# Rotary buffers and gathered v in a pool of their own, w_out staging moved, and the last stores of a hybrid encoder block in another order

## The chip, the cores and the metric

The kernel runs on one core of one Trainium2 chip. Its time is the device time of one execution in microseconds, and the median of several runs counts. The engines are named as in the profile: PE is TensorE's matmuls and PEld its weight loads, DVE is VectorE, ACT is ScalarE, POOL is GpSimd, SP is SyncE, which only issues DMAs. Each engine works through its own queue in order; engines wait for each other through semaphores.

## The reference

One layer: a projection into heads of two kinds, attention in both, a gate, a projection back, and a layer norm.

```python
h = x @ w_in                                   # 1024 x 1024 by 1024 x 3328
q_a, k_a, v_a, z_a, q_b, k_b, v_b, z_b = split(h)
y_a = neighborhood_attention(q_a, k_a, v_a, rel_bias)      # 8 heads, 8 x 16 windows on a 16 x 64 grid
y_b = windowed_gqa_with_sink(rotary(q_b), rotary(k_b), v_b, sink)   # 8 query heads, 2 kv heads, |i - j| <= 128
mixed = concat([y_a * silu(z_a), y_b * silu(z_b)])
x = layer_norm(ALPHA * x + mixed @ w_out) * gain + bias    # over rows of 1024, ALPHA = 2 ** 0.25
```

All inputs and the output are float32. x and the output are 1024 rows of 1024.

## The kernel before

Every large product is done in float16 pieces: an operand is scaled by a power of two and split into a high and a low half, and three matmuls (high by high, high by low, low by high) are summed in PSUM. The scale of a weight comes from the data, so weights are read twice in part: once for a sum of absolute values, once for the work.

The program falls into three stages.

**The head** computes v = x @ w_v for all tokens (`v_mms`, first four token tiles in float32r, the other four in float16 pieces) and then projects the first six column groups (`project`, ORDER[:6] = zb0, z0, kb, zb1, qb0, z1). It runs inside a `with` block that owns two pools, `vp` and `vw`; when the block is left their memory is free for the pools opened next. `vp` holds, in this order, the staging of x (tag `xr`, four buffers of 2 KB per partition) and two rings of three 2.6 KB buffers (tags `wvr` and `vt`), used first for raw w_v and then for the split v that is written to DRAM (`v_part`, L774, tile `vt`, DRAM tensor `vd`). `vw` holds eight tiles `v32` of 2.5 KB with v in float32, and then sixteen 2.5 KB tiles `wvh0`, `wvl0`, `wvh1`, ... `wvl7` with the split w_v. The last are read by the matmuls of the first phase alone, k = 7 last. `t_load` puts four raw blocks of w_out (`wot`) into such tiles, `t_add` combines them, and `t_store` writes the sums to DRAM (`tf`, L637).

The order of side work in the head is written by hand: `at(c, fn)` registers a function that runs after the c-th projection matmul, 48 matmuls for a group, 24 for each half of the tokens. `run_to` pumps matmuls and fires these events. `sum_w(i)` (L790, with its load at L724) sums the absolute values of the i-th of the 15 later weight groups, `w_scan` (L267) does so for the first six groups, and `w_scale(n)` turns the sums into a scale: one small matmul against ones (L273) and a chain of one-element operations on VectorE (L274 to L293). `w_scale(6)` serves all 15 later groups. `w_split` makes the halves of a weight: `hi` on ScalarE (L247), `lo` on GpSimd in two operations (L252, L253); each `lo` releases the next weight load on SP (L236). `wo_load` and `wo_scan` (L1043, L1049) read w_out for its scale.

The rotary embedding is `rope`: ScalarE copies a projected half into `rp_raw` (L383), VectorE shuffles it into `rp_sw` (L384), then two multiplies and an add (L385 to L387). Both are buffers of tag `va`. The result is split into keys (`split_k`, tiles `ks`) or queries (`split_q`, tiles `qs`).

Before the kb group ends, the pools are opened that follow `vp` and `vw` in the same memory: `rawp` (12 KB per partition), then `kq`. `kq` holds three tags: `va` (six buffers of 4.1 KB: rotary work here, later the gathered v, the bias tables and some blocks of w_out), `ks` (eight of 2 KB) and `qs` (two of 4 KB). Within a pool the tags lie in the order of their first use, so in `kq` it is `va`, `ks`, `qs`. `reuse_waits="tile"` makes a tile wait only for those earlier tiles whose memory it covers. After `kq` comes `ap` with the working tiles of the attention.

**The live stage** runs 128 attention units with the projections of the other 15 groups interleaved between them (`pump_to`), and a planner that places elementwise work on the engines by estimated costs and due times. Its order of instructions is fixed when the program is built.

**The end** (`final`) multiplies the gated heads by w_out in a scheme of seven products per 2 x 2 blocks, adds x (`add`, L1336), gathers row statistics (`bn`, L1348) and normalises eight blocks of 128 rows. Block t is done by `norm(t)`: for t = 7 ScalarE normalises all 1024 columns at once (L1414), then GpSimd multiplies by the gain (L1425), adds the bias (L1426) and SP stores the half (L1427), which is `norm_half`, called for both halves. The last block is row block 3 (`norm_last`): its right 512 columns and columns 384 to 511 go over VectorE (L1387, L1391) with stores on SP (L1393, L1395), its first 384 columns are multiplied by the gain on GpSimd (`norm_ahead`, L1367), then go through TensorE: an identity matmul (L1374) and two with the diagonal tiles `dm` and `ds` (L1383, L1384), and ScalarE, which also issues their store (L1394, L1396). Between the last product and these, TensorE runs matmuls on a tile of zeros (`warm`, L1373). The calls stand in this order at the end:

```python
c11(3)
norm_ahead(3)
norm_half(7, slice(0, 512))
norm_half(7, slice(512, 1024))
for c, tag in ((0, 256), "t"), ((256, 128), "s"), ((384, 128), "t"):
    add(3, 1, run("q3", 3, bank(tag), None, c), c, whole=True)
norm_last(3)
```

Of the kernel before, what the change touches and what calls it, by code (L numbers as in the profile page):

```python
# [7 lines left out]
F32 = mybir.dt.float32  # L8
# [4 lines left out]
AF = mybir.ActivationFunctionType  # L13
# [18 lines left out]
NPRO = 6  # L32
# [38 lines left out]
def hybrid_block(ctx, tc, xT, x, wt, wv, wo, bias, sink, gain, lbias, cos, sin, bmask, out):  # L71
    nc = tc.nc
# [10 lines left out]
    def bank(tag):  # L83
        bufs = {"pj": 2, "s": 4, "t": 2}[tag]
        return (ps1 if bufs == 1 else ps2).tile([128, 512], F32, tag=tag, name=f"ps_{tag}", bufs=bufs)
# [7 lines left out]
    def big_tile(name, shape=(128, 2, 512), dt=F32R):  # L93
        n = taken[0]
        taken[0] += 1
        tag = "big" if n < 8 or 16 <= n < 24 or n >= 32 + NS else "big2"
        return big.tile(list(shape), dt, tag=tag, name=name)

    xh, xl, x16h, x16l = {}, {}, {}, {}
    for half in range(2):  # L100
        for k in range(KT):
            t = big_tile(f"x{half}{k}", dt=F32 if half else F32R)
# [43 lines left out]
    raws, parts, tiles = {}, {}, {}  # L146
# [29 lines left out]
    def enq(eng, fn, *deps, prio=1, after=0, cost=None):  # L176
        op = Op(eng, fn, deps, prio, cost)
        if clock["step"] is not None:
            queues[eng].append(op)
        elif after:  # L180
            events.setdefault(ran[0] + after, []).append(op.emit)
        else:
            op.emit()
        return op
# [192 lines left out]
    def rope(ps, half):  # L377
        live = clock["step"] is not None
        sl = slice(512 * half, 512 * half + 512)
        eng, mul = ("pool", nc.gpsimd) if live else ("dve", nc.vector)  # L380
        raw = tiles["kq"].tile([128, 1024], F32, tag="va", name="rp_raw", bufs=6)[:, :512]
        sw = tiles["kq"].tile([128, 1024], F32, tag="va", name="rp_sw", bufs=6)[:, :512]
        o1 = enq("act", lambda: nc.scalar.activation(raw, ps, AF.Copy, scale=QSCALE), prio=0)  # L383
        o2 = enq("dve", lambda: nc.vector.stream_shuffle(sw, raw, SWAP), o1, after=2)  # L384
        o3 = enq(eng, lambda: mul.tensor_mul(raw, raw, tiles["cos"][:, sl]), o2, after=3)  # L385
        o4 = enq(eng, lambda: mul.tensor_mul(sw, sw, tiles["sin"][:, sl]), o2, after=3)
        o5 = enq(eng, lambda: mul.tensor_add(raw, raw, sw), o3, o4, after=4)  # L387
        return raw, o1, o5
# [86 lines left out]
    with ExitStack() as vctx:  # L475
        vp = vctx.enter_context(tc.tile_pool(name="vp", bufs=2))
        vw = vctx.enter_context(tc.tile_pool(name="vw", bufs=1))
# [146 lines left out]
        wot = {}  # L624

        def t_load():
            for n in range(4):
                t = vw.tile([128, 640], F32, tag=f"wv{'hl'[n % 2]}{n // 2}", name="wot")
                wot[n] = t[:, :512]
                nc.sync.dma_start(wot[n], wo[3, :, n])  # L630

# [163 lines left out]
        def at(c, fn, *a):  # L795
            events.setdefault(c, []).append(lambda: fn(*a))
# [5 lines left out]
            at(30 + 8 * t, v_part, t)  # L802
        for i in range(NS):
            at(14 + 14 * i + {11: 6, 13: -2, 14: -16}.get(i, 0), sum_w, i)
        at(224, w_scale, NPRO)
        for c, o in zip((20, 28, 68, 76), T_SUM):
            at(c, t_add, *o)
        at(90, t_store)
# [4 lines left out]
    rawp = ctx.enter_context(tc.tile_pool(name="rawp", bufs=1, reuse_waits="tile"))  # L813
    actx = ExitStack()
    tiles["kq"] = ctx.enter_context(tc.tile_pool(name="kq", bufs=4, reuse_waits="tile"))
    ap = actx.enter_context(tc.tile_pool(name="ap", bufs=3, reuse_waits="tile"))
    tiles["ap"] = ap

# [12 lines left out]
    va = {}  # L831

    def big_ap(shape, dt, name):
        return tiles["kq"].tile(shape, dt, tag="va", name=name, bufs=6)

    def gather_v(p):
        t = va[p] = big_ap([128, 8, 4 * VE], F16, f"va{p}")
# [479 lines left out]
    def final():  # L1317
# [15 lines left out]
        def add(t, a, ps, c=(0, 512), whole=False):  # L1333
            o, w = c
            xv = xrs[t][:, 512 * a + o:512 * a + o + w]
            nc.vector.scalar_tensor_tensor(xv, ps[:, o:o + w], yc, xv, op0=ALU.mult, op1=ALU.add)  # L1336
            finish()
            if whole:
                bn(t, a, c)
# [10 lines left out]
        def row_stats(t):  # L1350
            mv = fp.tile([128, 2], F32, tag="mv", name="mv")
            nc.vector.bn_aggr(mv, stats[t][:, :8 if t == 3 else 2, :])
            sd = fp.tile([128, 1], F32, tag="sd", name="sd")
            nc.scalar.activation(sd, mv[:, 1:2], AF.Sqrt, bias=eps)
            return mv, sd

        def row_scale(mv, sd):
            rstd = fp.tile([128, 1], F32, tag="rstd", name="rstd")
            nc.vector.reciprocal(rstd, sd)
            nmr = fp.tile([128, 1], F32, tag="nmr", name="nmr")  # L1360
            nc.vector.tensor_scalar(nmr, mv[:, 0:1], rstd, -1.0, op0=ALU.mult, op1=ALU.mult)
            return rstd, nmr
# [3 lines left out]
        def norm_ahead(t):  # L1366
            nc.gpsimd.tensor_mul(xrs[t][:, HP], xrs[t][:, HP], gb[:, HP])  # L1367

        def norm_last(t):
            ts = slice(128 * t, 128 * t + 128)  # L1370
            xr, pn = xrs[t], bank("t")
            for _ in range(40):
                nc.tensor.matmul(gq[:, :128], warm, warm, start=True, stop=True)  # L1373
            nc.tensor.matmul(pn[:, HP], identf, xr[:, HP], start=True, stop=False)  # L1374
            dm, ds = (fp.tile([128, 128], F32, name=n, bufs=1) for n in ("dm", "ds"))
            mv = fp.tile([128, 2], F32, tag="mv", name="mv")
            nc.vector.bn_aggr(mv, stats[t])
            sd = fp.tile([128, 1], F32, tag="sd", name="sd")
            nc.scalar.activation(dm, nident, AF.Copy, scale=mv[:, 0:1])
            nc.scalar.activation(sd, mv[:, 1:2], AF.Sqrt, bias=eps)  # L1380
            nc.scalar.activation(ds, identf, AF.Copy, scale=sd)
            rstd = fp.tile([128, 1], F32, tag="rstd", name="rstd")
            nc.tensor.matmul(pn[:, HP], dm, gb[:, HP], start=False, stop=False)  # L1383
            nc.tensor.matmul(pn[:, HP], ds, bb[:, HP], start=False, stop=True)  # L1384
            halves = (H1, gp, bp), (HQ, gq[:, 128:256], gq[:, 256:384])
            for h, g, _ in halves:
                nc.vector.scalar_tensor_tensor(xr[:, h], xr[:, h], mv[:, 0:1], g, op0=ALU.subtract, op1=ALU.mult)  # L1387
                if h is H1:
                    nc.vector.reciprocal(rstd, sd)
            for h, _, o in halves:  # L1390
                nc.vector.scalar_tensor_tensor(xr[:, h], xr[:, h], rstd, o, op0=ALU.mult, op1=ALU.add)  # L1391
                if h is H1:
                    nc.sync.dma_start(out[ts, h], xr[:, h])  # L1393
            nc.scalar.activation(xr[:, HP], pn[:, HP], AF.Copy, scale=rstd)  # L1394
            nc.sync.dma_start(out[ts, HQ], xr[:, HQ])  # L1395
            nc.scalar.dma_start(out[ts, HP], xr[:, HP])  # L1396
# [10 lines left out]
        def norm(t, *st_):  # L1407
            ts = slice(128 * t, 128 * t + 128)
            xr, ha, hb = xrs[t], slice(512, 1024), slice(0, 512)
            mv, sd = st_ or row_stats(t)  # L1410
            rstd, nmr = row_scale(mv, sd)
            both = t in (0, 4, 7)
            h = slice(0, 1024) if both else hb
            nc.scalar.activation(xr[:, h], xr[:, h], AF.Identity, bias=nmr, scale=rstd)  # L1414
            if not both:
                nc.vector.scalar_tensor_tensor(xr[:, ha], xr[:, ha], mv[:, 0:1], gp, op0=ALU.subtract, op1=ALU.mult)
                nc.vector.scalar_tensor_tensor(xr[:, ha], xr[:, ha], rstd, bp, op0=ALU.mult, op1=ALU.add)
                nc.sync.dma_start(out[ts, ha], xr[:, ha])
            for h in (ha, hb) if both else (hb,):
                if t != 7:  # L1420
                    norm_half(t, h)

        def norm_half(t, h):
            xr = xrs[t]
            nc.gpsimd.tensor_mul(xr[:, h], xr[:, h], gb[:, h])  # L1425
            nc.gpsimd.tensor_add(xr[:, h], xr[:, h], bb[:, h])  # L1426
            nc.sync.dma_start(out[128 * t:128 * t + 128, h], xr[:, h])  # L1427

# [52 lines left out]
        def c11(t):  # L1481
            add(t, 0, a[t], whole=True)
# [41 lines left out]
        p4(3)  # L1524
        q2(3)
        c11(3)
        norm_ahead(3)
        norm_half(7, slice(0, 512))
        norm_half(7, slice(512, 1024))
        for c, tag in ((0, 256), "t"), ((256, 128), "s"), ((384, 128), "t"):  # L1530
            add(3, 1, run("q3", 3, bank(tag), None, c), c, whole=True)
        norm_last(3)

    def m_last(between):
        z, za = zt[ZP[3][1]], zt[ZP[3][0]]
# [42 lines left out]
    for i in range(-LD, NU + LO):  # L1578
# [5 lines left out]
        per, h = divmod(i, 16)  # L1584
# [5 lines left out]
        if i in SCAN_LD:  # L1590
            n, b = divmod(NSCAN + SCAN_LD.index(i), 4)
# [9 lines left out]
        if i in B_LD:  # L1601
            n = B_LD.index(i)
            b_load(n, w_ops[NL - 5 + n] if n < 5 else b_ops[n - 5])
        if i in B_AT:
            n = B_AT.index(i)
# [51 lines left out]
        if 0 <= q < NU // 4:  # L1657
            g, p, j, h = quad(q)
# [93 lines left out]
```

## Time and profile before

| | |
|---|---|
| median of 3 runs | 440.08 us (439.59 to 440.48) |
| the profiled execution | 442.68 us, of which its span is 440.8 us |
| TensorE busy | 429.9 us (98%), 3209 matmuls |
| VectorE, ScalarE, GpSimd busy | 351.8, 316.3, 293.9 us |
| granted TensorE clock | 1.0 |
| DMA | 84.82 MB moved, mean 192 GB/s |

The profile page gives the busy time of each engine, its course in 40 slices, the DMA queues, the chain of waits that ended last, and the costliest groups of instructions. Times in the timeline are microseconds from the start of the span. Its rows give the start, the length, the engine, the line in the kernel, the operation, the tile written and those read, and their shapes; in brackets stands the time that the engine sat idle before and what ended that. A row of the chain gives start, length and what. Matmuls overlap each other in the pipeline: one of 512 columns lasts 0.38 us but the next starts after 0.22.

### The profile page before, as it was taken

The numbers are of one execution on the slowest core, as the hardware profiler recorded it, in microseconds if no ns is written. First come the engines' busy times: TensorE is split into PE (matmuls) and PEld (weight loads), VectorE is DVE, ScalarE is ACT, GpSimd is POOL, SyncE is SP. The second block draws the span as 40 slices with busy tenths as digits, with TensorE's granted clock in tenths as the row PEclk, the third lists the DMA queues.
The fourth block names the chain that finished last, engine by engine and source line by source line (L and its number), as shares of the span: only waits on it lengthen the run. The fifth ranks groups of instructions, "written<-read, shape, count | busy, mean of one in ns | idle before, by whom it ended". The sixth has DMA issues, their size and how long they took to land.

```text
span 440.8 us, 9457 instructions
## 1 busy us (share of the span) xinstructions
PE 429.9 (98%) x3209; PEld 250.9 (57%) x3209; DVE 351.8 (80%) x872; ACT 316.3 (72%) x682; POOL 293.9 (67%) x303
## 2 busy tenths in 40 slices
PE   9999999999999999999999999999999999999994
PEld 8997754444445655555565555555555655444453
DVE  5978966784987797898898998887888877787684
ACT  5849789669659887878897778879688883653122
POOL 0110085769468746978998899697689899358245
PEclk9999999999999999999999999999999999999999
DMA  7952479995448999988789999977999999923123
GB/s 259 406 187 60 124 236 331 259 328 192 134 141 175 197 159 237 189 166 147 126 188 198 221 191 185 235 176 136 241 177 210 159 169 293 402 86 137 48 75 117
DMA packets 131409, 84.82 MB, mean 192 GB/s; under 512 B 97568, under 2 KB 106656, under 8 KB 131360
## 3 DMA queue, kind: packets, MB, share of 16 engines
q1 hardware_dynamic: 131216, 84.02, 78.9%
q8 instruction: 25, 0.41, 0.4%
q14 instruction: 24, 0.20, 0.1%
q10 hardware_dynamic: 144, 0.20, 0.1%
HBM read 50.60 MB, written 10.52 MB: 139 GB/s over the span
## 4 chain that ended last, share of the span: by engine, by line
PE 58%; DVE 11%; issue 8%; ACT 8%; DMA 7%; POOL 6%; SPq 1%; POOLq 0%; DVEq 0%; ACTq 0%
PE ps_pj L449 21%; PE ps_s L556 6%; PE ps_t L991 5%; PE ps_pj L1300 5%; PE ps_t L1300 4%; PE ps_s L1300 4%; DMA wor<-in_wo 3%; PE ps_pj L556 3%; PE ps_t L556 3%; PE ps_s L914 2%; PE ps_s L915 2%; POOL wl L253 2%; DVE split L963 2%; ACT ps_s L944 1%; DMA T<-td 1%
## 5 line engine op out<-in xcount | busy, mean ns | idle before, releaser
L449 PE MATMUL ps_pj<-xf,wh 128*128 128x512 f16 x672 | 201.3, 379 | 0.3 <-DVE z L414 0.3
L449 PE MATMUL ps_pj<-xf,wl 128*128 128x512 f16 x336 | 127.3, 379 | 0.0
L449 PEld LDWEIGHTS <-wh 128*128 128x128 f16 x672 | 63.7, 98 | 59.8 <-issue 1.8
L944 ACT ACTIVATE ps_s<-sn,nm 128x321 f32<-128x321 f32 (+3 forms) x128 | 67.7, 529 | 35.4 <-DVE nm L928 34.4
L963 DVE SCALAR_TENSOR_TENSOR split<-ps_s,split 128x320 f16<-128x320 f32 (+2 forms) x128 | 62.7, 490 | 23.3 <-ACT split L962 22.1
L252 POOL TENSOR_SCALAR wr<-wr,wsc 128x512 f32<-128x512 f32 x32 | 23.7, 741 | 61.6 <-ACT wh L247 59.0
L962 ACT ACTIVATE split<-ps_s 128x320 f16<-128x320 f32 (+2 forms) x128 | 55.0, 430 | 1.6
L449 PEld LDWEIGHTS <-wl 128*128 128x128 f16 x336 | 32.8, 98 | 38.0
L253 POOL TENSOR_TENSOR wl<-wr,wh 128x512 f16<-128x512 f32 x32 | 39.9, 1247 | 2.7
L914 PE MATMUL ps_s<-ks,qs 128*128 128x320 f16 (+3 forms) x128 | 38.1, 298 | 1.7 <-DVE split L963 1.7
L915 PE MATMUL ps_s<-ks,qs 128*128 128x320 f16 (+3 forms) x128 | 38.2, 298 | 0.0
L991 PEld LDWEIGHTS <-tr 128*128 128x128 f16 (+1 forms) x1056 | 36.2, 98 | 3.3 <-issue 1.2
L928 DVE CUSTOM_DVE_ANT_0 sn<-ps_s,bias,sg 128x368 f32<-128x368 f32 (+1 forms) x64 | 36.1, 564 | 2.1 <-PE ps_s L915 2.0
L928 DVE CUSTOM_DVE_ANT_0 sn<-ps_s,bm,nsk 128x320 f32<-128x320 f32 (+2 forms) x64 | 36.5, 571 | 0.4
L1300 PEld LDWEIGHTS <-m 128*128 128x128 f16 x186 | 17.6, 98 | 19.9 <-POOL m L1222 0.5
L366 POOL COPY ks<-ks 64x512 f16<-64x512 f16 x40 | 25.8, 644 | 3.9 <-ACT ks L310 1.7
L1425 POOL TENSOR_TENSOR xr<-xr,gb 128x512 f32<-128x512 f32 x10 | 12.7, 1270 | 20.2 <-ACT xr L1414 20.2
L247 ACT ACTIVATE wh<-wr,wsc 128x512 f16<-128x512 f32 x32 | 22.7, 710 | 1.6 <-DVE wsc L277 1.6
L556 PEld LDWEIGHTS <-xf 128*128 128x128 f16 x192 | 18.6, 98 | 7.3
L915 PEld LDWEIGHTS <-qs 128*128 128x128 f16 x128 | 12.5, 98 | 17.4 <-issue 3.2
L914 PEld LDWEIGHTS <-qs 128*128 128x128 f16 x128 | 12.5, 98 | 15.2 <-DVE qs L318 0.2
L991 PE MATMUL ps_t<-va,tr 128*128 128x65 f16 (+1 forms) x528 | 19.2, 193 | 0.3 <-DMA tr<-split 0.3
(262 smaller groups left out, 949.1 us busy)
## 6 DMA issues: line engine op xcount, KB each, us to landing
wr<-in_wt SPq DMA_DIRECT2D x32, 256.0 KB, 3.3
ws<-in_wt SPq DMA_DIRECT2D x15, 512.0 KB, 6.5
wor<-in_wo SPq DMA_DIRECT2D x20, 256.0 KB, 3.9
xr<-in_x SPq DMA_DIRECT2D x8, 512.0 KB, 9.1
out<-xr SPq DMA_DIRECT2D x15, 256.0 KB, 2.0
bias<-in_bias SPq DMA_DIRECT2D x8, 440.0 KB, 4.4
wob<-in_wo SPq DMA_DIRECT2D x12, 256.0 KB, 4.0
wvraw<-in_wv SPq DMA_DIRECT2D x9, 320.0 KB, 5.6
```

What stands on the lines that cost most here:

```text
L253: nc.gpsimd.tensor_sub(l, raw, h)
L366: nc.gpsimd.tensor_copy(place(t, o, half, col), place(t, a, half, col))
L449: nc.tensor.matmul(ps, a[:, k % 4, :], mv, start=(k == 0 and i == 0), stop=(k == KT - 1 and i == 2))
L556: nc.tensor.matmul(ps[:, :320], lh[:, ts], rh[:, cs], start=(k == ko[0] and i == 0), stop=(k == ko[-1] and i == 2))
L914: nc.tensor.matmul(ps[:, :n], q, sl[0], start=True, stop=False)
L915: nc.tensor.matmul(ps[:, :n], q, sl[1], start=False, stop=True)
L928: nc.vector.tensor_tensor_reduce(sn[:, at0:at0 + n], ps[:, :n], bias_t, sg[:, c:c + 1], init, op0=ALU.add, op1=ALU.min, accum_out=nm)
L944: nc.scalar.activation(pt[:, c], sn[:, c], AF.Exp, bias=nm, scale=-1.0, accum_out=acc)
L962: nc.scalar.activation(h, pt[:, c], AF.Copy, scale=PSCALE)
L963: nc.vector.scalar_tensor_tensor(l, pt[:, c], PSCALE, h, op0=ALU.mult, op1=ALU.subtract)
L991: nc.tensor.matmul(ps[:, w * m:w * m + e], a, b_, start=(i == 0), stop=(i == len(mms) - 1))
L1300: nc.tensor.matmul(ps[:, cs], lh[:, 128 * t:128 * t + 128], rh[:, cs], start=(fresh and e == 0 and n == 0), stop=(e == len(terms) - 1 and ...
```

## The change

Five edits go together.

1. The tag `va` moves from `kq` into a pool of its own, `va`, which is opened right after `kq`. `kq` then holds keys and queries alone, at the start of the freed memory behind `rawp`, and the rotary buffers lie above them. The sum of both is as large as `kq` was.
2. The raw w_out blocks `wot` are loaded into the tiles of `wvh6`, `wvl6`, `wvh7` and `wvl7` in place of those of `wvh0` to `wvl1`.
3. `w_scale` for the 15 later groups runs after matmul 217 of the head, not after 224.
4. For block 7, ScalarE normalises columns 0 to 511 and 512 to 1023 in two operations, the left ones first. `norm_ahead(3)` stands between the multiply and the add of block 7's left half, and the right half of block 7, its store included, comes behind `norm_last(3)`.
5. `norm_last` runs 28 warm matmuls, not 40.

```diff
--- before.py
+++ after.py
@@ -378,8 +378,8 @@
         live = clock["step"] is not None
         sl = slice(512 * half, 512 * half + 512)
         eng, mul = ("pool", nc.gpsimd) if live else ("dve", nc.vector)
-        raw = tiles["kq"].tile([128, 1024], F32, tag="va", name="rp_raw", bufs=6)[:, :512]
-        sw = tiles["kq"].tile([128, 1024], F32, tag="va", name="rp_sw", bufs=6)[:, :512]
+        raw = tiles["va"].tile([128, 1024], F32, tag="va", name="rp_raw", bufs=6)[:, :512]
+        sw = tiles["va"].tile([128, 1024], F32, tag="va", name="rp_sw", bufs=6)[:, :512]
         o1 = enq("act", lambda: nc.scalar.activation(raw, ps, AF.Copy, scale=QSCALE), prio=0)
         o2 = enq("dve", lambda: nc.vector.stream_shuffle(sw, raw, SWAP), o1, after=2)
         o3 = enq(eng, lambda: mul.tensor_mul(raw, raw, tiles["cos"][:, sl]), o2, after=3)
@@ -625,7 +625,7 @@
 
         def t_load():
             for n in range(4):
-                t = vw.tile([128, 640], F32, tag=f"wv{'hl'[n % 2]}{n // 2}", name="wot")
+                t = vw.tile([128, 640], F32, tag=f"wv{'hl'[n % 2]}{6 + n // 2}", name="wot")
                 wot[n] = t[:, :512]
                 nc.sync.dma_start(wot[n], wo[3, :, n])
 
@@ -802,7 +802,7 @@
             at(30 + 8 * t, v_part, t)
         for i in range(NS):
             at(14 + 14 * i + {11: 6, 13: -2, 14: -16}.get(i, 0), sum_w, i)
-        at(224, w_scale, NPRO)
+        at(217, w_scale, NPRO)
         for c, o in zip((20, 28, 68, 76), T_SUM):
             at(c, t_add, *o)
         at(90, t_store)
@@ -813,6 +813,7 @@
     rawp = ctx.enter_context(tc.tile_pool(name="rawp", bufs=1, reuse_waits="tile"))
     actx = ExitStack()
     tiles["kq"] = ctx.enter_context(tc.tile_pool(name="kq", bufs=4, reuse_waits="tile"))
+    tiles["va"] = ctx.enter_context(tc.tile_pool(name="va", bufs=6, reuse_waits="tile"))
     ap = actx.enter_context(tc.tile_pool(name="ap", bufs=3, reuse_waits="tile"))
     tiles["ap"] = ap
 
@@ -831,7 +832,7 @@
     va = {}
 
     def big_ap(shape, dt, name):
-        return tiles["kq"].tile(shape, dt, tag="va", name=name, bufs=6)
+        return tiles["va"].tile(shape, dt, tag="va", name=name, bufs=6)
 
     def gather_v(p):
         t = va[p] = big_ap([128, 8, 4 * VE], F16, f"va{p}")
@@ -1369,7 +1370,7 @@
         def norm_last(t):
             ts = slice(128 * t, 128 * t + 128)
             xr, pn = xrs[t], bank("t")
-            for _ in range(40):
+            for _ in range(28):
                 nc.tensor.matmul(gq[:, :128], warm, warm, start=True, stop=True)
             nc.tensor.matmul(pn[:, HP], identf, xr[:, HP], start=True, stop=False)
             dm, ds = (fp.tile([128, 128], F32, name=n, bufs=1) for n in ("dm", "ds"))
@@ -1411,7 +1412,8 @@
             rstd, nmr = row_scale(mv, sd)
             both = t in (0, 4, 7)
             h = slice(0, 1024) if both else hb
-            nc.scalar.activation(xr[:, h], xr[:, h], AF.Identity, bias=nmr, scale=rstd)
+            for h in (hb, ha) if t == 7 else (h,):
+                nc.scalar.activation(xr[:, h], xr[:, h], AF.Identity, bias=nmr, scale=rstd)
             if not both:
                 nc.vector.scalar_tensor_tensor(xr[:, ha], xr[:, ha], mv[:, 0:1], gp, op0=ALU.subtract, op1=ALU.mult)
                 nc.vector.scalar_tensor_tensor(xr[:, ha], xr[:, ha], rstd, bp, op0=ALU.mult, op1=ALU.add)
@@ -1420,9 +1422,11 @@
                 if t != 7:
                     norm_half(t, h)
 
-        def norm_half(t, h):
+        def norm_half(t, h, between=None):
             xr = xrs[t]
             nc.gpsimd.tensor_mul(xr[:, h], xr[:, h], gb[:, h])
+            if between:
+                between()
             nc.gpsimd.tensor_add(xr[:, h], xr[:, h], bb[:, h])
             nc.sync.dma_start(out[128 * t:128 * t + 128, h], xr[:, h])
 
@@ -1524,12 +1528,11 @@
         p4(3)
         q2(3)
         c11(3)
-        norm_ahead(3)
-        norm_half(7, slice(0, 512))
-        norm_half(7, slice(512, 1024))
+        norm_half(7, slice(0, 512), lambda: norm_ahead(3))
         for c, tag in ((0, 256), "t"), ((256, 128), "s"), ((384, 128), "t"):
             add(3, 1, run("q3", 3, bank(tag), None, c), c, whole=True)
         norm_last(3)
+        norm_half(7, slice(512, 1024))
 
     def m_last(between):
         z, za = zt[ZP[3][1]], zt[ZP[3][0]]
```

## The prediction

> **What bounds the kernel now.** I read the page first, then the chain of waits over the last 16 us, then the timeline of the same stretch, and at last the waits of TensorE in the first 130 us, where the other parts of the change lie.
>
> ```profile
> span 440.8 us, 9457 instructions
> PE 429.9 (98%) x3209; PEld 250.9 (57%) x3209; DVE 351.8 (80%) x872; ACT 316.3 (72%) x682; POOL 293.9 (67%) x303
> ```
>
> TensorE is busy for 429.9 of 440.8 us, so an edit pays only where it closes one of the few holes in front of a matmul, or where TensorE has ended. The end comes first. The chain of waits (start, length, what) shows what holds it:
>
> ```profile
> 430.69 0.99 POOL xr L1367
> 431.68 1.24 POOL xr L1425
> 432.99 1.26 POOL xr L1426
> 434.25 1.24 POOL xr L1425
> ```
>
> From 430.69 on it is GpSimd alone: `norm_ahead(3)` (L1367), then multiply (L1425) and add (L1426) for each half of row block 7. The timeline (start, length, engine, line; in brackets the idle time before) has the rest:
>
> ```profile
> 425.36 0.81 ACT L1414 ACTIVATE xr<-xr,nmr,rstd 128x512 f32<-128x512 f32 x1 [0.48 <-DVE nmr L1361]
> ...
> 426.25 1.27 POOL L1425 TENSOR_TENSOR xr<-xr,gb 128x512 f32<-128x512 f32 x1 [2.61 <-ACT xr L1414]
> ...
> 429.27 1.24 ACT L1414 ACTIVATE xr<-xr,nmr,rstd 128x1024 f32<-128x1024 f32 x1 [0.48 <-DVE nmr L1361]
> ...
> 430.41 2.40 PE L1373 MATMUL ps_s<-warm 128*128 128x128 f16 x40
> ...
> 432.64 0.86 PE L1374 MATMUL ps_t<-xr,identf 128*128 128x384 f32 x2
> ...
> 433.76 0.91 PE L1383 MATMUL ps_t<-gb,dm 128*128 128x384 f32 x2 [0.26 <-ACT dm L1379]
> ...
> 434.29 1.00 DVE L1391 SCALAR_TENSOR_TENSOR xr<-xr,rstd,ps_s 128x512 f32<-128x512 f32 x2
> ...
> 435.56 1.26 POOL L1426 TENSOR_TENSOR xr<-xr,bb 128x512 f32<-128x512 f32 x1
> 436.01 0.37 ACTq L1396 DMA_DIRECT2D out<-xr  x1
> 437.28 0.43 SPq L1393 DMA_DIRECT2D out<-xr  x1
> 437.80 0.41 SPq L1395 DMA_DIRECT2D out<-xr  x1
> ```
>
> Row block 3, the last to be normalised, is finished on VectorE at 435.29 (434.29 + 1.00), yet its two stores leave at 437.28 and 437.80: they stand on SP behind block 7's second half, whose add ends at 436.82. The last store goes out 2.5 us after its data is there, and the issues' table says when it lands:
>
> ```profile
> out<-xr SPq DMA_DIRECT2D x15, 256.0 KB, 2.0
> ...
> out<-xr ACTq DMA_DIRECT2D x1, 192.0 KB, 1.9
> ...
> out<-xr SPq DMA_DIRECT2D x1, 64.0 KB, 2.0
> ```
>
> 437.80 + 2.0 = 439.8, and 1.0 us later the span ends.
>
> **The tail, step by step.** ScalarE now takes block 7 in two pieces of 512. The first starts at 429.27 as before and takes 0.81, so it ends at 430.08; GpSimd follows 0.08 behind (425.36 + 0.81 to 426.25): 430.16. Its five operations keep their durations in a new order: multiply 1.27 (to 431.4), `norm_ahead` 0.99 (432.4), add 1.26 (433.7), multiply 1.27 (434.9), add 1.26 (436.2, with small gaps). The second piece on ScalarE, done by about 430.9, is needed at 433.7. On SP the order becomes block 7 first half (433.7), block 3 right half (data at about 435.0), its 128 columns (435.3), block 7 second half (436.2). Nothing queues behind that last one. Its landing is 436.2 + 2.0 = 438.2; ScalarE's store of block 3's first 384 columns lands at 436.01 + 1.9 = 437.9, just before. So the last landing comes 1.6 us sooner (437.80 against 436.2), and beyond 0.3 us the ScalarE store would be late next. I take 1.6. Bounds: 2.5 us if the data of block 3 alone counted (437.80 − 435.3), nothing if that other store slips.
>
> By the Trainium skill, page "DMA: Bandwidth & Descriptors", section "Anatomy of one DMA — SWDGE (gpsimd) path", one transfer costs about 2.0 us fixed plus its bytes at 436 GB/s; that speaks against the change, since the last store would now carry 256 KB and not 64 KB and be some 0.45 us slower (an estimate from that page), leaving about 1.15 us of gain. The rows above have 2.0 us for both sizes; I go by them.
>
> The twelve warm matmuls that go free 12/40 of 2.40, 0.7 us, of TensorE: the first matmul behind them now finds `norm_ahead` done at 432.4 and starts at about 432.5 in place of 432.64. That buys nothing, since L1383 waits for ScalarE's `dm` until 433.76 either way; the cut only makes room for `norm_ahead`, which ends 0.7 later than before (432.4 against 431.68). Were `dm` not the later one, that 0.7 would reach ScalarE's store.
>
> **The head: pools, staging, w_scale.** In KB per partition above the start of the freed pools: row staging 0–8, wv/vt rings 8–23.4, the eight v32 23.4–43.5, sixteen wv tiles 43.5–83.5. `rawp` covers 0–12. Before, the rotary buffers came next (12–36.4), then keys and queries. Now keys and queries lie at 12–36 and rotary at 36–60.4, over the last v32 and the first seven wv tiles. The timeline, with two rows of the chain (91.54 and 109.43), the share of the DMA engines in a window (its last pair) and one row of the issues' table:
>
> ```profile
> 88.97 0.60 ACT L383 ACTIVATE rp_raw<-ps_pj 128x512 f32<-128x512 f32 x1 [3.44 <-DMA vd<-vt]
> ...
> 90.23 0.16 PE L273 MATMUL ps_t<-wm,ones 128*128 128x2 bf16 x1 [0.45 <-ACT junk L267]
> ...
> 91.54 5.76 DMA ws<-in_wt
> ...
> 95.34 0.61 ACT L312 CAST ks<-rp_raw 64x512 f16<-64x512 f32 x1 [0.43 <-DMA tf<-wot]
> ...
> 97.38 1.06 ACT L790 ACTIVATE junk<-ws 128x1024 bf16<-128x1024 f32 x1 [1.43 <-DMA ws<-in_wt]
> ...
> 99.19 0.71 ACT L247 ACTIVATE wh<-wr,wsc 128x512 f16<-128x512 f32 x1
> ...
> 101.14 0.16 PE L273 MATMUL ps_t<-wm,ones 128*128 128x2 bf16 x1 [0.36 <-ACT junk L267]
> ...
> 101.25 0.69 POOL L252 TENSOR_SCALAR wr<-wr,wsc 128x512 f32<-128x512 f32 x1
> ...
> 105.06 0.71 ACT L247 ACTIVATE wh<-wr,wsc 128x512 f16<-128x512 f32 x1
> ...
> 106.61 0.70 POOL L252 TENSOR_SCALAR wr<-wr,wsc 128x512 f32<-128x512 f32 x1
> ...
> 107.81 0.18 ACT L790 ACTIVATION_READ_ACCUMULATOR junk<-ws 128x1 f32 x1
> ...
> 109.36 0.17 PE L273 MATMUL ps_t<-wm,ones 128*128 128x15 bf16 x1
> ...
> 109.43 4.50 DMA wor<-in_wo
> ...
> 123.28 0.25 PE L915 MATMUL ps_s<-ks,qs 128*128 128x192 f16 x1
> 123.83 0.59 PE L449 MATMUL ps_pj<-xf,wh 128*128 128x512 f16 x2 [0.30 <-DVE z L414]
> ...
> 90.00:95.00 5.00, 4.77 (x23) 2.17 (x23) 4.74 (x12) 4.19 (x9) 1.64 (x2) 1.00 1.06 307
> ...
> vd<-vt SPq DMA_DIRECT2D x16, 130.0 KB, 6.3
> ```
>
> *Rotary.* ScalarE, free 3.44 us earlier, may write `rp_raw` only at 88.97, when a store of a vt buffer lying under it has landed. Over v32 and wv, which no DMA reads, that wait goes, and ScalarE is up to 3.4 us ahead. TensorE's hole at 90.23 (0.45) closes. What is late next: ScalarE's queue comes to the sum of `ws` at 97.38, which waits for a transfer, issued at 91.54 in a stretch whose DMA engines are full (share 1.06); ScalarE being early does not move it. All behind it in ScalarE's queue stays, so the hole at 101.14 grows by what 90.23 gave back. Net 0 there.
>
> GpSimd, though, is relieved: `wh` and the keys' copies move ahead, so the split at 101.25 can start right after `wh` (99.19 + 0.71), 1.3 us sooner, and the one at 106.61 after `wh` at 105.06 + 0.71, at 105.8: 0.8 sooner. SP's next load, and the `wor` load behind it (109.43), go 0.8 sooner, then ScalarE's scan, the second qb0 rotary on VectorE and the evacuation z, for which TensorE waits at 123.83. That hole is 0.30 by its row; what is lost is 0.47, since the matmul at 123.28 with its 0.25 overlaps the next one, due 0.08 behind it.
>
> *w_scale.* Seven matmuls earlier is 7 × 0.21 = 1.5 us (23 matmuls in 4.77 us, the window's row): about 107.85 in place of 109.36. It reads the last sum, done at 107.99, so TensorE, with every projection behind it, waits 0.15 to 0.2 us; at most 1.5, as any longer wait stood at 109.36 already. In return its VectorE chain runs before the first qb0 rotary, not between the two, so the second can really start 0.8 sooner. Together the head gives 0.47 − 0.2 = 0.3, between −1.0 (0.47 − 1.5) and +0.5.
>
> *Staging.* The four wo loads wait for the last matmuls on wv tiles 6 and 7:
>
> ```profile
> 33.39 0.31 PE L556 MATMUL ps_t<-wvl,x 128*128 128x320 f32 x1
> ...
> 33.76 3.27 SPq L596 DMA_DIRECT2D wvraw<-in_wv  x2
> ...
> 42.14 0.82 ACT L599 ACTIVATE wq<-wvraw,runit 128x640 f16<-128x640 f32 x1
> ```
>
> The last two leave at 33.7 and 34.1 (an issue takes up to 0.43); behind them on SP stands the wv reload of 33.76, which slips to 34.4, +0.7. It is read at 42.14; even the slow 6.3 us of a vd store would land it at 40.7. Hidden, 0; without that cover 0.7. Keys over the vt rings: were their write at 95.34 to wait for the last vd store (issued 90.2, + 6.3 = 96.5), two casts of 0.61 would end at 97.7, 0.3 past 97.38; I take 0.
>
> **Sum.** 1.6 + 0.3 = 1.9 us. The profiled execution took 442.68 us in all with its span of 440.8: the span becomes 438.9, the whole 440.8. Against the median of the runs, 440.08, which lies 2.6 below the profiled one, the same 1.9 gives **438.2**. 0.2%, 0.88 us, is about what a measurement of this kernel can tell from no change.
>
> **Rivals.**
> - *The head gives more.* If the 97.38 sum does come earlier (its transfer released by work that is now done sooner), the holes of 0.45 and 0.36 at L273 close, each with some 0.15 of overlap as at 123.83, about 1.1 more: 437.1. For it: the transfer is issued at 91.54, after the time at which ScalarE falls behind. Against: the DMA engines are full.
> - *The head only loses.* GpSimd's relief does not reach 123.83 and w_scale waits up to 0.5: 440.08 − 1.6 + 0.5 = 439.0.
> - *The tail does not do what it says.* Another store takes its place: block 3's by ScalarE slips 1 us or more, or the four stores within 2.5 us delay one another. Then the end gives 0.5 and the head 0: 439.6.
> - *Slower.* The rotary buffers meet memory that is freed still later than the vt ring, as the key tiles did at 95.34 with the wo store. ScalarE has up to 6.5 us of work between 88.97 and 97.38 (8.4 less its waits of 1.43 and 0.43), so a release after 90.9 delays 97.38 and all behind it one for one; at 95.3 that is 4.4: 440.08 + 4.4 − 1.6 = 442.9. It turns the sign from 92.5 on. Against it: wo's staging has moved to 73.5–83.5 KB, beyond 60.4, so no DMA reads what lies under the rotary buffers.
>
> **How the numbers follow.** Forecast (437.6 to 438.7) 0.66; head more (436.8 to 437.6) 0.08; head loses (438.7 to 439.2) 0.12; tail hidden (439.2 to 440.4) 0.09; slower 0.05. The range 437.4 to 439.3 leaves out the last two and part of the second. Faster by over 0.2% are the first three, 0.86; the same 0.09; slower 0.05.
>
> **What would show it.** In the changed profile the last SP store is L1427's, issued near 436.2 less what the head gained, about 1 to 1.5 us behind the L1393 store; GpSimd goes L1425, L1367, L1426 without a hole. `rp_raw` starts within 0.2 of its matmuls' end; the L273 hole near 90 is gone and that near 101 about 1 us wide; w_scale's matmul shows a hole of 0.1 to 0.3; the z hole near 123.8 is gone. A last store from ScalarE, an `rp_raw` that still waits on a DMA, or L790 well before 97 would make me wrong.

## The result, and the profile after

The changed kernel takes 438.34 us (median of 9 runs, 436.47 to 439.2) where the kernel before takes 440.47 (9 runs, 439.35 to 442.04): a ratio of 0.9945, with a 95% interval of 0.9925 to 0.9965. That is 2.1 us less; 1.9 was forecast. The profiled execution took 439.2 us, 437.3 of them its span, so it lies 0.9 above its median as the one of before lay 2.2 above the median of these runs. A comparison of the two spans (3.5 us) therefore says too much, and below each stage is measured against a mark of its own. The pages give a span to 0.1 us, so a difference taken from one is good to 0.05.

The end first, in the timeline (start, length, engine, line; in brackets the idle time before). Behind the diff's first additions the lines count one more than before, `norm_half` two or four more: L1367 is now L1368, L1425 to L1427 are L1427, L1430 and L1431, L1393 to L1396 are L1394 to L1397.

```profile
427.88 1.27 POOL L1427 TENSOR_TENSOR xr<-xr,gb 128x512 f32<-128x512 f32 x1 [1.29 <-ACT xr L1416]
428.13 1.73 PE L1374 MATMUL ps_s<-warm 128*128 128x128 f16 x28
429.10 1.00 POOL L1368 TENSOR_TENSOR xr<-xr,gb 128x384 f32<-128x384 f32 x1
430.05 1.27 POOL L1430 TENSOR_TENSOR xr<-xr,bb 128x512 f32<-128x512 f32 x1
431.28 1.28 POOL L1427 TENSOR_TENSOR xr<-xr,gb 128x512 f32<-128x512 f32 x1
431.47 0.91 PE L1384 MATMUL ps_t<-gb,dm 128*128 128x384 f32 x2 [0.40 <-ACT dm L1380]
432.64 1.26 POOL L1430 TENSOR_TENSOR xr<-xr,bb 128x512 f32<-128x512 f32 x1
432.77 0.33 SPq L1394 DMA_DIRECT2D out<-xr  x1
433.19 0.38 SPq L1396 DMA_DIRECT2D out<-xr  x1
433.73 0.37 ACTq L1397 DMA_DIRECT2D out<-xr  x1
433.93 0.33 SPq L1431 DMA_DIRECT2D out<-xr  x1
```

The reader sees GpSimd in the new order without a hole, block 3's stores at 432.77 and 433.19 no longer behind block 7's second half, and that half as the last store, at 433.93. The whole end lies 2.28 us earlier than in the trace of before (the warm matmuls start at 428.13 and not at 430.41), so 433.93 is the foretold 436.2. The issues' table of the stretch from 433.7 on (KB each, median us to landing) shows what went otherwise:

```profile
out<-xr SPq DMA_DIRECT2D x1, 256.0 KB, 2.4
out<-xr ACTq DMA_DIRECT2D x1, 192.0 KB, 2.0
```

The last store lands after 2.4 us and not after 2.0. From the start of the warm matmuls to the end of the span it is 437.3 − 428.13 = 9.17 us; in the trace of before it is 440.8 − 430.41 = 10.39. The end gives 1.2 us.

Now the head, in the timeline of the stretch from 85 to 124 us:

```profile
85.30 0.60 ACT L383 ACTIVATE rp_raw<-ps_pj 128x512 f32<-128x512 f32 x1 [0.41 <-PE ps_pj L449]
90.50 0.60 ACT L383 ACTIVATE rp_raw<-ps_pj 128x512 f32<-128x512 f32 x1 [0.19 <-PE ps_pj L449]
91.81 0.69 POOL L252 TENSOR_SCALAR wr<-wr,wsc 128x512 f32<-128x512 f32 x1 [1.30 <-ACT wh L247]
97.38 1.06 ACT L790 ACTIVATE junk<-ws 128x1024 bf16<-128x1024 f32 x1 [4.53 <-DMA ws<-in_wt]
101.13 0.16 PE L273 MATMUL ps_t<-wm,ones 128*128 128x2 bf16 x1 [1.60 <-ACT junk L267]
102.01 0.34 SPq L236 DMA_DIRECT2D wr<-in_wt  x1
105.93 0.69 POOL L252 TENSOR_SCALAR wr<-wr,wsc 128x512 f32<-128x512 f32 x1 [0.57 <-POOL ks L366]
108.04 0.17 PE L273 MATMUL ps_t<-wm,ones 128*128 128x15 bf16 x1
111.77 0.63 ACT L1050 ACTIVATE junk<-wor 128x512 bf16<-128x512 f32 x1 [2.08 <-DMA wor<-in_wo]
114.32 0.72 DVE L384 STREAM_SHUFFLE rp_sw<-rp_raw 128x512 f32<-128x512 f32 x1
123.47 0.25 PE L916 MATMUL ps_s<-ks,qs 128*128 128x192 f16 x1
123.55 0.59 PE L449 MATMUL ps_pj<-xf,wh 128*128 128x512 f16 x2
```

The first `rp_raw`, which had waited for a store until 88.97, starts at 85.30, and the second at 90.50; each waits for its own matmuls alone. The hole of 0.45 near 90 is gone. The sum L790 still starts at 97.38, now after 4.53 us of waiting for its transfer, and the hole at 101 has taken in what was gained ahead of it. The projection behind the first qb0 scores starts 0.08 after them (123.47 to 123.55), without the 0.30 it waited for z.

### The profile page after: what moved, and what is told of

Same layout as the page of the kernel before. It is cut to its first block, busy times and chain, and to the rows that moved or that the text cites. A ratio compares the mean times of both kernels' runs of the same rounds, so it can differ in the third digit from the quotient of the medians.

```text
span 437.3 us, 9430 instructions
## 1 busy us (share of the span) xinstructions
PE 427.8 (98%) x3197; PEld 249.1 (57%) x3197; DVE 350.6 (80%) x872; ACT 316.4 (72%) x683; POOL 293.4 (67%) x303
## 4 chain that ended last, share of the span: by engine, by line
PE 57%; DVE 12%; POOL 8%; issue 8%; ACT 7%; DMA 5%; SPq 1%; POOLq 0%; DVEq 0%; ACTq 0%
PE ps_pj L449 30%; PE ps_t L992 5%; PE ps_pj L1301 4%; PE ps_t L1301 3%; PE ps_s L556 3%; PE ps_s L915 3%; PE ps_s L916 3%; PE ps_s L1301 2%; DVE xm L564 2%; DMA ws<-in_wt 2%; PE ps_pj L556 2%; PE ps_t L556 1%; DVE split L964 1%; POOL tp L1098 1%; POOL wl L253 1%
## 5 line engine op out<-in xcount | busy, mean ns | idle before, releaser
L252 POOL TENSOR_SCALAR wr<-wr,wsc 128x512 f32<-128x512 f32 x32 | 22.7, 710 | 59.5 <-ACT wh L247 55.0
L366 POOL COPY ks<-ks 64x512 f16<-64x512 f16 x40 | 26.7, 667 | 4.0 <-ACT ks L310 1.2
L1427 POOL TENSOR_TENSOR xr<-xr,gb 128x512 f32<-128x512 f32 x10 | 12.7, 1271 | 21.6 <-ACT xr L1416 21.6
L556 PEld LDWEIGHTS <-xf 128*128 128x128 f16 x192 | 18.5, 98 | 7.5 <-issue 0.3
```

The lines of the kernel that those rows point to most:

```text
L366: nc.gpsimd.tensor_copy(place(t, o, half, col), place(t, a, half, col))
L556: nc.tensor.matmul(ps[:, :320], lh[:, ts], rh[:, cs], start=(k == ko[0] and i == 0), stop=(k == ko[-1] and i == 2))
```

## The experiments

**The end alone.** The kernel before with the last stores in their new order and 28 warm matmuls; the head is the old one.

```diff
-            for _ in range(40):
+            for _ in range(28):
...
-            nc.scalar.activation(xr[:, h], xr[:, h], AF.Identity, bias=nmr, scale=rstd)
+            for h in (hb, ha) if t == 7 else (h,):
+                nc.scalar.activation(xr[:, h], xr[:, h], AF.Identity, bias=nmr, scale=rstd)
...
-        norm_ahead(3)
-        norm_half(7, slice(0, 512))
-        norm_half(7, slice(512, 1024))
+        norm_half(7, slice(0, 512), lambda: norm_ahead(3))
...
         norm_last(3)
+        norm_half(7, slice(512, 1024))
```

> Only the edits at the end (block 7 in two pieces on ScalarE, the new order of its halves and of norm_ahead, 28 warm matmuls) on the kernel before. Theory: the last store is issued about 1.6 us sooner after the last product than before, but lands 2.4 and not 2.0 us later, because ScalarE's store of 192 KB has left 0.2 us ahead of it; so the span from the start of the warm matmuls to the end shrinks from 10.4 to about 9.2 us, and the whole time by 1.2 us, 439.2. The holes in front of L273 at 90 and 101 us stay as before (0.45 and 0.36). Rival: the whole gain of the change (2.1 by the medians, 3.5 by the two profiled executions) comes from the end, then this is 438.3 or less.

Measured: 439.68 us (11 runs) against 440.63 (24 runs), a ratio of 0.9973 (0.9958 to 0.9988): 1.2 us less. In the trace the warm matmuls start at 427.92 and the span ends at 437.1, 9.18 us, as in the full change. So the end is worth the same 1.2 us with the old head and with the new one, and it is the larger part of the whole. This trace also shows the old head once more, with two holes near 123:

```profile
122.48 0.26 PE L914 MATMUL ps_s<-ks,qs 128*128 128x192 f16 x1 [0.38 <-DVE qs L318]
123.20 0.59 PE L449 MATMUL ps_pj<-xf,wh 128*128 128x512 f16 x2 [0.38 <-DVE z L414]
```

**The head alone.** The pools, the staging of the raw wo blocks and the place of `w_scale` as changed, the end as before.

```diff
-        raw = tiles["kq"].tile([128, 1024], F32, tag="va", name="rp_raw", bufs=6)[:, :512]
+        raw = tiles["va"].tile([128, 1024], F32, tag="va", name="rp_raw", bufs=6)[:, :512]
...
-                t = vw.tile([128, 640], F32, tag=f"wv{'hl'[n % 2]}{n // 2}", name="wot")
+                t = vw.tile([128, 640], F32, tag=f"wv{'hl'[n % 2]}{6 + n // 2}", name="wot")
...
-        at(224, w_scale, NPRO)
+        at(217, w_scale, NPRO)
...
+    tiles["va"] = ctx.enter_context(tc.tile_pool(name="va", bufs=6, reuse_waits="tile"))
...
```

> Only the edits of the first 125 us (pool of the rotary buffers, w_out staging, w_scale after matmul 217) on the kernel before. Theory: the hole near 90 goes, the one near 101 grows by as much, because ScalarE's queue is held until 97.3 by the transfer of one weight group; w_scale's matmul shows 0.03 to 0.2, the hole at 123.8 goes; net 0.3 us, 440.1. The holes at 169 to 182 and 318 us stay about as they are (2.2 and 0.9 us together). Rival: the head also closes the holes at 169 to 182 and 318, which the changed kernel's profile no longer shows in full; then it is worth 1.5 to 2, 438.5 to 439.

Measured: 440.02 us (12 runs), a ratio of 0.9991 (0.9973 to 1.0008): 0.4 us less, between 1.2 less and 0.4 more. The other way to the same number, the full change against the end alone (0.9945 against 0.9973), gives 0.28%, 1.2 us, with some 1.1 us on either side. Both hold the 0.3 of the forecast, and neither shows more than that the head costs nothing to speak of; what it gains these runs do not settle. The trace has no hole left at 123, and the one at 101 is 0.83 us wide here:

```profile
100.19 0.16 PE L273 MATMUL ps_t<-wm,ones 128*128 128x2 bf16 x1 [0.83 <-ACT junk L267]
```

The rival, that the head also closes later holes, is not borne out: the longest wait between 169 and 182 us is 0.84 us here and 0.88 in the trace of the end alone. The hole near 318 shows in neither of the two. In the changed kernel the first is 0.25, with the same head as here, so the head alone does not decide it.

**`w_scale` back at matmul 224**, the rest as changed:

```diff
-        at(217, w_scale, NPRO)
+        at(224, w_scale, NPRO)
```

> The changed kernel with w_scale back after matmul 224. Theory: w_scale's matmul no longer waits, but its 2.4 us of VectorE operations stand between the two qb0 rotaries again, so the second rotary starts 0.4 to 0.5 us later than in the changed kernel and the hole before the matmul after the first attention unit (near 123.6) opens to 0.1 to 0.3 us; the time is the changed kernel's plus 0 to 0.3, 438.5. Rival: the move was worth nothing or cost what it waits, 0.2, then 438.1 to 438.3.

Measured: 438.45 us (7 runs), a ratio of 0.9956 (0.9938 to 0.9974), the same as the full change. In the timeline the second qb0 rotary now stands behind the scale's chain and starts at 114.40:

```profile
113.01 0.58 ACT L383 ACTIVATE rp_raw<-ps_pj 128x512 f32<-128x512 f32 x1
114.40 0.73 DVE L384 STREAM_SHUFFLE rp_sw<-rp_raw 128x512 f32<-128x512 f32 x1
121.74 0.69 DVE L414 SCALAR_TENSOR_TENSOR z<-z,ps_pj 128x512 f32<-128x512 f32 x1
123.00 0.59 PE L449 MATMUL ps_pj<-xf,wh 128*128 128x512 f16 x2
```

Its `rp_raw` was done at 113.59, so the rotary lost 0.8 us to the chain; in the changed kernel it follows 0.04 behind `rp_raw` (114.28 to 114.32). But z is done at 122.43, 0.57 before TensorE needs it at 123.00, and no hole near 123 opens. The move of `w_scale` is worth nothing that these runs can tell.

**The raw wo blocks back in wv's first tiles**, the rest as changed; the first tiles now lie under the rotary buffers.

```diff
-                t = vw.tile([128, 640], F32, tag=f"wv{'hl'[n % 2]}{6 + n // 2}", name="wot")
+                t = vw.tile([128, 640], F32, tag=f"wv{'hl'[n % 2]}{n // 2}", name="wot")
```

> The changed kernel with the raw wo blocks back in wv's first tiles, so that the store of them (tf<-wot, landed at 95.3 us in the profile of before) reads memory that now lies under the rotary buffers. My theory (a rotary buffer waits for the transfer that reads what lay under it): the second rp_raw, 90.50 in the changed kernel, starts at about 95.2; behind it 0.6, a split of 0.7 and two casts of 0.6 make 97.8, so the sum at 97.38 slips 0.4 and TensorE with it: +0.4 us against the changed kernel, about 438.7 (0 to +0.8), the z hole near 123.8 open again in part. Rival (the move of the blocks is bookkeeping only): rp_raw stays at 90.5 and the time at 438.3.

Measured: 441.45 us (12 runs) against 440.94 (17 runs of the kernel before in a second series, on another chip), a ratio of 1.0024 (1.0004 to 1.0043). Against the ratio of the full change that is 0.8%, 3.5 us, all of its gain and more. The mechanism that I named is there, but the price went another way than I had reckoned:

```profile
94.07 0.60 ACT L383 ACTIVATE rp_raw<-ps_pj 128x512 f32<-128x512 f32 x1 [3.69 <-DMA tf<-wot]
95.37 0.69 POOL L252 TENSOR_SCALAR wr<-wr,wsc 128x512 f32<-128x512 f32 x1 [4.86 <-ACT wh L247]
96.44 1.06 ACT L790 ACTIVATE junk<-ws 128x1024 bf16<-128x1024 f32 x1
104.77 0.34 SPq L236 DMA_DIRECT2D wr<-in_wt  x1
113.36 0.63 ACT L1050 ACTIVATE junk<-wor 128x512 bf16<-128x512 f32 x1 [4.28 <-DMA wor<-in_wo]
123.97 0.26 PE L915 MATMUL ps_s<-ks,qs 128*128 128x192 f16 x1 [1.27 <-DVE qs L318]
124.68 0.59 PE L449 MATMUL ps_pj<-xf,wh 128*128 128x512 f16 x2 [0.38 <-DVE z L414]
```

The second `rp_raw` waits for the store of the wo blocks until 94.07 (90.50 in the changed kernel). The sum L790 does not slip at all: it starts at 96.44, straight behind ScalarE's casts, 0.94 sooner than in the changed kernel, since its transfer has landed by then in this trace. But `wh` stands behind `rp_raw` on ScalarE, so GpSimd's split slips from 91.81 to 95.37, and with it SP's next weight loads, which wait for the split's second half:

```profile
SPq L236 <- POOL wl L253: 9.4, 2, 6.2
```

(the waits of SP from 85 to 107 us: total, times, longest; in the changed kernel the total is 5.7). The load at 102.01 goes at 104.77, the `wor` load stands behind it, ScalarE's scan slips from 111.77 to 113.36, the second qb0 rotary stands behind it, and TensorE waits 1.27 for queries and 0.38 for z. Up to matmul 640 TensorE is 0.85 us ahead of the changed kernel's trace (108.29 against 109.14), at matmul 720 it is 1.13 behind (127.06 against 125.93): between the two this chain costs 2.0 us, and 1.1 is left when the earlier L790 is set against it. The profiled spans differ by 1.3, the ratios by 3.5 us with some 1.2 on either side. Part of that gap is that this profiled execution lies 1.0 below its median and that of the changed kernel 0.9 above its own; where the rest of the 3.5 lies, these single traces do not show.

**The sum of weight group 10 later**, at matmul 170 in place of 154, the rest as changed; in the changed kernel it is the sum that holds ScalarE until 97.38.

```diff
-            at(14 + 14 * i + {11: 6, 13: -2, 14: -16}.get(i, 0), sum_w, i)
+            at(14 + 14 * i + {10: 16, 11: 6, 13: -2, 14: -16}.get(i, 0), sum_w, i)
```

> The changed kernel with the absolute sum of weight group 10 run after matmul 170 of the head, not 154, so that it stands behind the two scans that the w_scale matmul near 101 us waits for. Theory (ScalarE's queue, held by that sum's transfer until 97.3, is what pins the hole): the hole of 1.6 us near 101 falls to under 0.3, since the scan's own weight lands at about 96; the later sums and loads follow, and TensorE is 1.0 to 1.7 us ahead from there to the end, 436.6 to 437.3. Rival 1: the DMA engines pin it all the same (the scan's weight or the later sums land too late, w_scale's matmul at 108 waits instead): 438.3. Rival 2: the hole closes but the live stage gives it back in the holes after 169 us: 438.3 with TensorE ahead only until there.

Measured: 436.94 us (6 runs, 435.49 to 437.9), a ratio of 0.9924 (0.9907 to 0.9941). That is 1.4 us below the changed kernel by the medians, but 0.9 by the ratios with some 1.2 on either side; against the kernel with `w_scale` at 224, which ran in the same series, it is 1.4 with 1.1 on either side. The hole near 101 is gone:

```profile
92.61 0.63 ACT L267 ACTIVATE junk<-wr 128x512 bf16<-128x512 f32 x1
99.10 0.17 PE L273 MATMUL ps_t<-wm,ones 128*128 128x2 bf16 x1
...
368.55 1.47 PE L1301 MATMUL ps_t<-T,m 128*128 128x512 f16 x6 [1.12 <-DMA T<-td]
```

The scan L267 that TensorE waits for runs at 92.61 and not behind a sum that waits for its transfer, and the small matmul, now at 99.10, has no idle time ahead of it. What ate the gain of the early `rp_raw` in the changed kernel was therefore the order of ScalarE's queue, a sum that waits in front of a scan. TensorE reaches matmul 640 2.17 us sooner than in the changed kernel (106.97 against 109.14); two later holes, of 0.77 us at 353.24 for GpSimd and of 1.12 at 368.55 for a transfer (0.56 in the changed kernel), take a part back.

**That, and the last add shared.** VectorE adds columns 768 to 1023 of block 7, GpSimd columns 512 to 767.

```diff
-        norm_half(7, slice(512, 1024))
+        x7 = xrs[7]
+        nc.gpsimd.tensor_mul(x7[:, H1], x7[:, H1], gb[:, H1])
+        for eng, h in (nc.vector, slice(768, 1024)), (nc.gpsimd, slice(512, 768)):
+            eng.tensor_add(x7[:, h], x7[:, h], bb[:, h])
+        nc.sync.dma_start(out[896:1024, H1], x7[:, H1])
```

> The changed kernel with the sum of weight group 10 at matmul 170 in place of 154, and the last add of block 7's second half shared: VectorE, idle from 433.0 on, adds columns 768 to 1023, GpSimd columns 512 to 767 (0.65 in place of 1.26). My theory: the last SP store leaves some 0.5 us sooner, ScalarE's store of 192 KB, which left 0.2 us ahead of it, becomes the last; from the start of the warm matmuls to the end of the span 8.6 to 9.0 us in place of 9.21, the median 436.94 less 0.4: 436.5. Rival (GpSimd and VectorE slow one another in these adds, or the four stores still land together): 9.1 to 9.3, 436.9.

Measured: 436.7 us (6 runs) against 440.94, a ratio of 0.9913 (0.9888 to 0.9938): the fastest kernel of the study, though not apart from the one above. The timeline and the issues' table of its last two stores:

```profile
424.83 1.73 PE L1374 MATMUL ps_s<-warm 128*128 128x128 f16 x28
429.34 0.72 POOL L1538 TENSOR_TENSOR xr<-xr,bb 128x256 f32<-128x256 f32 x1
429.63 0.72 DVE L1538 TENSOR_TENSOR xr<-xr,bb 128x256 f32<-128x256 f32 x1
430.41 0.38 SPq L1539 DMA_DIRECT2D out<-xr  x1
430.44 0.37 ACTq L1397 DMA_DIRECT2D out<-xr  x1
```

```profile
out<-xr SPq DMA_DIRECT2D x1, 256.0 KB, 2.4
out<-xr ACTq DMA_DIRECT2D x1, 192.0 KB, 2.6
```

The SP store leaves 5.58 us behind the start of the warm matmuls in place of 5.80, and ScalarE's store is the last, but now that one takes 2.6 us. The end is 434.0 − 424.83 = 9.17 us, as long as with the add on GpSimd alone. The rival held: the four stores land together, and the sharing gave nothing that shows. What is gained over the changed kernel comes from the head.

**Without ScalarE's last store**, so that block 3's first 384 columns are not written:

```diff
-            nc.scalar.dma_start(out[ts, HP], xr[:, HP])
```

> The changed kernel without ScalarE's last store (block 3's first 384 columns are not written). Theory (the last store lands after 2.4 us and not 2.0 because it shares the engines with the 192 KB that left 0.2 us ahead): the last store lands 2.0 us after its issue, and from the start of the warm matmuls to the end of the span it is 8.8 us in place of 9.21. Rival (the last 256 KB are slower for another reason, the SP stores ahead of them or their size): still 2.4, and 9.2.

This kernel ran once, with a span of 436.6 us. The timeline, and the issues' table from 433.5 on:

```profile
427.81 1.73 PE L1374 MATMUL ps_s<-warm 128*128 128x128 f16 x28
433.62 0.33 SPq L1430 DMA_DIRECT2D out<-xr  x1
```

```profile
out<-xr SPq DMA_DIRECT2D x1, 256.0 KB, 2.0
```

The last store leaves as far behind the warm matmuls as in the changed kernel (5.81) and lands after 2.0; the end is 436.6 − 427.81 = 8.79 us. The 0.4 us is what ScalarE's store, 0.2 us ahead, costs the last one.

**40 warm matmuls again**, the rest as changed:

```diff
-            for _ in range(28):
+            for _ in range(40):
```

> The changed kernel with 40 warm matmuls again in place of 28. Theory (the cut is worth nothing, because TensorE waits for ScalarE's dm anyway): the hole of 0.30 in front of the identity matmuls goes, that in front of the dm matmuls shrinks to about 0.1 to 0.2, and from the start of the warm matmuls to the end of the span it stays 9.2 us. Rival (the end of the warm matmuls passes on to ScalarE's store): 9.4 to 9.9.

This kernel, too, ran once. The hole ahead of the `dm` matmuls shrinks from 0.40 to 0.25, and the end is 437.1 − 427.86 = 9.24 us, the same as with 28 within the rounding of the spans. The cut of the warm matmuls is worth nothing, as foretold.

```profile
427.86 2.40 PE L1374 MATMUL ps_s<-warm 128*128 128x128 f16 x40
431.20 0.91 PE L1384 MATMUL ps_t<-gb,dm 128*128 128x384 f32 x2 [0.25 <-ACT dm L1380]
```

## Why the prediction was right, and where it was not

The sum was 1.6 + 0.3 = 1.9 us against 2.1 measured (438.2 against 438.34). That the two agree so well is in part luck: the end gave 0.4 less than forecast, what the head gave lies anywhere from −0.4 to some 2.3 us by the two ways of taking it, and 438.2 was reckoned from a median of 440.08, which nine runs put at 440.47. The steps came out as follows.

*The order of the end* is right to the instruction: GpSimd's five operations without a hole, block 3's stores free, the last store 1.6 us sooner relative to the warm matmuls. *Its size* is the term that was mis-sized: 1.6 forecast, 1.2 measured. From the start of the warm matmuls the end takes 9.17 to 9.25 us in every trace with the new order and all its stores, 10.39 and 10.42 in the two with the old one. The step that failed is the landing of the last store, for which I took 2.0 from the row of fifteen 256 KB stores. That row is a median over the whole run. The same table of before, for 436.7 to 437.1 and for 437.2 to 437.5, had the warning:

```profile
out<-xr SPq DMA_DIRECT2D x1, 256.0 KB, 2.1
...
out<-xr SPq DMA_DIRECT2D x1, 256.0 KB, 2.3
```

The second is the store of 437.28, which left 0.4 us behind the first, block 7's second half. The 64 KB half a microsecond behind it are not the likely cause: in the changed kernel 256 KB leave at 432.77 with 64 KB 0.42 behind, and land in 2.0. The last store of the changed kernel leaves 0.2 us behind 192 KB, which costs 0.4 us; without them it lands in 2.0.

With the fixed and variable parts of the Trainium skill, page "DMA: Bandwidth & Descriptors", section "Anatomy of one DMA — SWDGE (gpsimd) path", the prediction estimated 1.15 for this term, and 1.2 was measured, but not for that reason. The page gives these parts for transfers that GpSimd issues, and the last store of either kernel leaves from SP: 256 KB with nothing 0.2 us ahead land in 2.0 us here, 64 KB in 1.8 to 2.0. What fits the runs is the Trainium skill, the same page, section "Queues, rings and completion order": SP's and ScalarE's rows are served in turn by the same 16 engines. The run without ScalarE's store agrees, 2.0 in place of 2.4. It does not show that two queues are needed for it, since the 2.3 above stands behind a store of the same queue.

*The rotary buffers* did what was said: no wait on a transfer, the hole near 90 gone, L790 no sooner, the hole at 101 wider. It is 1.60 in this trace and not 1, since TensorE also came 0.94 us sooner out of the first 8 us of this execution than in that of before, which is no part of the change, and the transfer swallowed that too. In the four other traces with the new pools and staging and the sum in its old place the hole is 0.53 to 1.42 wide. That L790 starts at 97.38 in both traces is chance: in those four it starts at 96.43 to 97.25, and with the old head and the new end at 96.13. At matmul 640 the two traces stand at 109.14 both; at matmul 720 the changed one is 0.27 ahead, where 0.3 was the sum of the head. One pair can't show so little: at matmul 720 the two traces with the old head stand at 125.57 and 126.20, those five with the new one at 124.98 to 125.93.

*GpSimd's relief* is right: the second split starts at 105.93 where 105.8 was foretold, and the holes at 123 to 124, which both traces with the old head show (0.30; 0.38 twice), are gone in all seven traces with the full change's pools and staging. The reverse run, with the wo blocks back, is the stronger witness: the same chain from `rp_raw` over GpSimd, SP's loads, the scan and the rotary to TensorE, in the other direction, costs 2.0 us between matmuls 640 and 720. *w_scale* is half right: TensorE loses about 0.2 us at 108.04 as foretold (the matmul ahead starts at 107.63, and 0.22 is the usual step). The return is there too ("so the second can really start 0.8 sooner"): with `w_scale` at 224 that rotary stands 0.8 behind its `rp_raw`. But it brings TensorE nothing, as z is in time without it.

*Staging* was costed at nothing for SP's queue, and nothing shows. Yet of the four parts it is the one that decides the sign: without it the rest of the change makes the kernel 0.24% slower (0.04 to 0.43%). The rival that I called slower has its mechanism shown by that run; it was its price that I had wrong, then and in the expectation. By its rule a release at 94.07 would have put L790 off by 3.2 us (94.07 − 90.9), and L790 started at 96.44; only 2.4 us of ScalarE's work stood between this `rp_raw` and L790, not the 6.5 that I had put there, and I followed ScalarE's queue alone and not what GpSimd and SP pass on.

## What to carry to other kernels

A buffer that moves to other memory inherits the waits of what lay there, so move the old tenants' transfers together with it, and price a late release along every queue that passes it on, not only the one it stands in. An engine that is made earlier gains little while its queue has an instruction ahead that waits for a transfer, here 4.53 us of it; reorder that queue first. The landing of the last stores of a kernel is read from the stretch where they leave together, not from a median over all stores.

## What was not expected of the hardware

Stores that leave close together slow one another. On two queues, within 0.03 to 0.2 us, 256 KB took 2.4 us and 192 KB up to 2.6, where 256 KB without the other queue's store took 2.0; on one queue, 256 KB 0.4 us behind 256 KB took 2.3. VectorE and GpSimd adding 256 columns at once took 0.72 us each.

TensorE's speed in the first 8 us differs from run to run of the same instructions. The timeline of TensorE has this row in the trace of before

```profile
6.46 0.47 PE L556 MATMUL ps_s<-wvh,x 128*128 128x320 f32 x1
```

and this one in that of the changed kernel:

```profile
5.21 0.31 PE L556 MATMUL ps_s<-wvh,x 128*128 128x320 f32 x1
```

The matmul L556 still takes 0.47 us at 6.46 in the one and 0.31 at 5.21 in the other, 17 matmuls against 21 between 3.3 and 6.6 us, under a granted clock that reads 1.00 in both. The first of them to take under 0.35 us starts at 6.98 in the trace of before, at 4.30 in that of the changed kernel, and between 4.21 and 6.98 in all ten. The 40th matmul stood 0.1 to 1.1 us earlier in the traces of the nine other kernels than in that of before. The Trainium skill, page "TensorE: Matmul & The Clock Gate", section "Part 1: The HAM clock gate", has the time of such a step vary by half a microsecond either way, with where in a free-running window the first matmul falls; the spread here, 2.8 us, is wider, and the clock in the rows does not show the step, so no run here ties it to that window. The spread of the 40th matmul is as large as the head's whole effect, and one profile of each kernel can't tell the two apart.
